# Where the split weights lie in their buffers: rows of 136 floats against rows of 128 with a start that steps

## The chip, the cores and the metric

The program runs on one core of one Trainium2 chip. The metric is the device time of one execution in microseconds; the kernel before took 2110.36 us (median of three runs, 2109.91 to 2113.37).

Names of the engines: PE is TensorE (matmuls), PEld the weight loads that it runs beside them, DVE is VectorE, ACT ScalarE, POOL GpSimd, SP SyncE, which issues the DMAs of the weights.

## What is computed

A two-layer encoder trunk on 256 tokens of width 2048, in float32. Each layer is a norm, an attention mixer with its projections, and a squared-ReLU MLP:

```python
for i in range(DEPTH):
    h = rms_norm(x, attn_norm[i])
    if i % 2 == 0:
        x = x + even_mixer(h, even_w_in[j], even_rpb[j], even_w_out[j])
    else:
        x = x + odd_mixer(h, odd_w_qkv[j], odd_sink[j], odd_w_out[j])
    x = x + sq_relu_mlp(rms_norm(x, mlp_norm[i]), w_mlp_in[i], w_mlp_out[i])
return rms_norm(x, final_norm)
```

Nearly all the work is the product of 256 tokens with weight matrices, 382 MB of which come in from HBM once.

## The kernel before

**Units.** Weights come as units of 128 output columns by 2048 inputs, in two halves of eight 128x128 blocks each. `take_half` issues the DMA of a half unit into a buffer `r` (six of them), and `split` makes two parts of it: `h`, the value rounded to float32r, by ACT (line 82), and `l = r - h`, by DVE (line 83). Each part has a pool of five buffers (`whi`, `wlo`).

**Pairs.** The activations (`u`, `hid` or `o`) are split the same way and lie as [128, k, 2, 256]: for each k the high part and behind it the low part, 2048 bytes together. `k_range` runs, for each k, one pair of matmuls into the same PSUM tile `acc`: block `h[k]` as the weights with 512 moving columns (line 150), and block `l[k]` with the 256 columns of the high part (line 152). Each matmul loads its own weights, and the load of the next runs beside the matmul before it. Pairs follow each other without a break, 16 to a unit: the projections, the MLP's two products (`hid` has 32 k for a unit of its second one), and the output projections.

**Value passes.** In `value_pair` the roles are turned: blocks of `u` are the weights, and 256 columns of `h` or `l` move (line 272), 96 matmuls to a pass and ten passes. The buffers of these half units are filled without gaps (`flat=True`).

**Rows.** All other half units are written into rows of `ROW = P + 8` = 136 floats, 544 bytes, of which 512 are used. Twelve units have the last two blocks of their second half in small tiles of their own, `hh` and `hl`, where rows of 128 floats follow each other without gaps; they belong to the two or three units that a projection begins with (`some_units`), whose last two pairs run at the end, one unit's after another's.

**Addresses.** In the built program, within a partition, `u` begins at byte 32896, `hid` and `o` at 160768, the five `h` buffers at 99744 and then every 4352 bytes, the five `l` buffers at 121504 and then every 4352, and all `hh` and `hl` tiles lie at 160 past a multiple of 256. What matters below is the place modulo 256: 128 for `u`, 0 for `hid` and `o`, 160 for every `h` and `l` buffer (4352 is 17 times 256), and the 2048-byte rows of the activations do not change it. Row k of a weight buffer begins 544k bytes in, so its place moves on by 32 with each k, and `h[k]` and `l[k]` have the same place. The **distance** of a block is its place less that of the moving operand, modulo 256: with `u` it runs 32, 64, 96 … 224, 0 over the eight k of a half unit, with `hid` and `o` it runs 160, 192, 224, 0 … 128; `hh` and `hl` stand at 32 with `u` and at 160 with `o` for both of their rows.

What sets the order: SP, ACT, DVE and PE each run their instructions as written, with `AHEAD = 2` half units loaded ahead of the one in use; attention steps are put between units by a list of tasks counted in ticks of four k.

Of the kernel before, what the change touches and what calls it, by code (L numbers as in the profile page):

```python
# [8 lines left out]
F32R = mybir.dt.float32r  # L9
# [5 lines left out]
P = 128  # L15
T = 256
# [8 lines left out]
SCALE = 128.0 ** -0.5  # L25
TW = 384
HALF = KT // 2
ROW = P + 8
RAW_BUFS = 6
PART_BUFS = 5  # L30

# [10 lines left out]
def encoder(ctx: ExitStack, tc: tile.TileContext, a: dict, outT: bass.AP):  # L42
# [4 lines left out]
    whi = ctx.enter_context(tc.tile_pool(name="whi", bufs=PART_BUFS))  # L47
    wlo = ctx.enter_context(tc.tile_pool(name="wlo", bufs=PART_BUFS))
# [32 lines left out]
    def split(hi, lo, src):  # L81
        nc.scalar.activation(hi, src, AF.Copy)  # L82
        nc.vector.tensor_sub(lo, src, hi.bitcast(F32))  # L83
# [3 lines left out]
    pending = []  # L87
    loaded = []

    def need(units, held=0, flat=False):  # L90

        for i, src in enumerate(units):
            pending.extend([(src[:, :HALF, :], HALF, flat),
                            (src[:, HALF:, :], HALF - 2 if i < held else HALF, flat)])

    def take_half():
        while pending and len(loaded) <= AHEAD:
            src, n, flat = pending.pop(0)
            r = raw.tile([P, HALF, P], F32, name="r")
            nc.sync.dma_start(r, src)  # L100
            h = whi.tile([P, HALF, ROW], F32R, name="h")
            l = wlo.tile([P, HALF, ROW], F32R, name="l")
            if flat:
                h, l = (w.rearrange("p k c -> p (k c)")[:, :HALF * P] for w in (h, l))
                split(h, l, r.rearrange("p k c -> p (k c)"))
                loaded.append((h, l, None))
                continue
            h, l = h[:, :, :P], l[:, :, :P]
            split(h[:, :n, :], l[:, :n, :], r[:, :n, :])
            tiles = [(h[:, k, :], l[:, k, :]) for k in range(n)]  # L110
            if n < HALF:
                h, l = (held_w.tile([P, 2, P], F32R, name=name) for name in ("hh", "hl"))
                split(h, l, r[:, n:, :])
                tiles += [(h[:, k, :], l[:, k, :]) for k in range(2)]
            loaded.append((h, l, tiles))
        return loaded.pop(0)

    def take_unit():
        return take_half()[2] + take_half()[2]
# [13 lines left out]
    def tick():  # L133
        now[0] += 1
        run_due()
# [49 lines left out]
    def gained(k, which):  # L185
        x, gk = xs[:, k, :], g[:, which, k:k + 1]
        if which == 4:
            nc.scalar.activation(x, x, AF.Copy, scale=gk)
        else:
            nc.scalar.activation(u[:, k, 0, :], x, AF.Copy, scale=gk)  # L190
            nc.vector.scalar_tensor_tensor(u[:, k, 1, :], x, gk, u[:, k, 0, :].bitcast(F32),
                                           op0=ALU.mult, op1=ALU.subtract)
# [68 lines left out]
    def value_pair(pool, keep):  # L261

        ps = acc_ps.tile([P, 2, T], F32, name="acc")
        for half in range(2):
            parts = [take_half()[:2] for _ in range(2)]
            for kk in range(HALF):
                k = half * HALF + kk
                h, l = (w[:, (kk % 4) * T:(kk % 4 + 1) * T] for w in parts[kk // 4])
                for j in range(2):
                    js = slice(j * P, (j + 1) * P)  # L270
                    for n, (x, y) in enumerate(((0, h), (0, l), (1, h))):
                        nc.tensor.matmul(ps[:, j, :], u[:, k, x, js], y,  # L272
                                         start=k == 0 and j == 0 and n == 0,
                                         stop=k == KT - 1 and n == 2, skip_group_check=True)
                if kk % 2 == 1:
                    tick()
        assert norm["ready"]
        w = pool.tile([P, 2, 2, T], F32R, name="v", bufs=1)
        for j in range(2):
            nc.scalar.activation(w[:, 0, j, :], ps[:, j, :], AF.Copy, scale=rcol[:, j:j + 1])  # L280
            nc.vector.scalar_tensor_tensor(w[:, 1, j, :], ps[:, j, :], rcol[:, j:j + 1],
                                           w[:, 0, j, :].bitcast(F32), op0=ALU.mult, op1=ALU.subtract)
        keep.append(w)
# [131 lines left out]
    for p in range(8):  # L415
        base = 2 * p if p < 4 else 24 + 2 * (p - 4)
        for i in range(2):
            need([w0[base + i], w0[base + 8 + i]])
        need([a["even_w_v"][p, i] for i in range(2)], flat=True)
    need([a["even_w_out"][c] for c in range(KT)], 3)  # L420

    def mlp_units(layer):
# [5 lines left out]
    mlp_units(0)  # L428
    for p in range(2):
        need([w1[NH + 2 * p + i] for i in range(2)], 2 if p == 0 else 0)  # L430
        need([a["odd_w_v"][p, i] for i in range(2)], flat=True)
        need([w1[8 * p + i] for i in range(8)])
    need([a["odd_w_out"][c] for c in range(KT)], 3)
    mlp_units(1)
# [7 lines left out]
    STARTERS = 3  # L442
# [14 lines left out]
    hl = [None] * STARTERS  # L457
    for k0, k1 in GROUPS:
        ks = slice(k0 % HALF, (k1 - 1) % HALF + 1)
        if k0 % HALF == 0:  # L460
            hl = [(whi.tile([P, HALF, ROW], F32R, name="h")[:, :, :P], wlo.tile([P, HALF, ROW], F32R, name="l")[:, :, :P])
                  for _ in range(STARTERS)]
        for i in range(STARTERS):
            split(hl[i][0][:, ks, :], hl[i][1][:, ks, :], rs[k0 // HALF][i][:, ks, :])
            if i == 0:
                for k in range(k0, k1):
                    gained(k, 0)
        for i in range(STARTERS):
            h, l = hl[i]
            for k in range(k0, k1):  # L470
                nc.tensor.matmul(sps[i], h[:, k % HALF, :], u[:, k].rearrange("p a t -> p (a t)"),
                                 start=k == 0, stop=False)
                nc.tensor.matmul(sps[i][:, :T], l[:, k % HALF, :], u[:, k, 0, :], start=False, stop=k == KT - 1)
# [12 lines left out]
    with tc.tile_pool(name="attn0", bufs=1) as pool:  # L486
# [24 lines left out]
        for p in range(8):  # L511
            q, k, v = [[], []], [[], []], []
            for i in range(2):
                for j, (dst, name, sc) in enumerate(((q, "q", SCALE), (k, "k", 1.0))):
                    done = head_parts(pool, name, 2, sc, dst[i])
                    if p == 0 and 2 * i + j < STARTERS:
                        done(sps[2 * i + j])
                    else:
                        unit(done, u)
                h = 2 * p + i  # L520
                attend(pool, o, h, q[i], k[i], v, i,
                       grid_bias(h) if h < 8 else toeplitz(pool, sl[h - 8], 1), LAGS_0)
            if p < 3:
                for h in range(2 * p + 2, 2 * p + 4):
                    make_grid_bias(h)
            value_pair(pool, v)
# [5 lines left out]
    with tc.tile_pool(name="attn1", bufs=1) as pool:  # L532
        o = pool.tile([P, NH, 2, T], F32R, name="o")
        sl = slopes(16)
        for p in range(2):
            k, v = [[], []], []
            done = [head_parts(pool, "k", 2, 1.0, k[i]) for i in range(2)]
            if p == 0:
                some_units(done, u)
                later(2, norm_for_heads)  # L540
            else:
                for i in range(2):
                    unit(done[i], u)
            value_pair(pool, v)
            for i in range(8):
                h = 8 * p + i
                q = []
                unit(head_parts(pool, "q", 2, SCALE, q), u)
                attend(pool, o, h, q, k[i // 4], v, i // 4, toeplitz(pool, sl[h], 2),
                       LAGS_1 if h < NH - 3 else LAGS_END, True)  # L550
        project_out(o, 3)
        finish_tasks()
# [87 lines left out]
```

## Time and profile before

| | us |
|---|---|
| median of 3 runs | 2110.36 |
| the profiled execution | 2113.29 |
| its span, first to last instruction | 2111.4 |
| PE busy | 2088.1 |
| DVE busy | 1339.8 |
| ACT busy | 1036.6 |

A line of the page's groups reads: source line, engine, operation, tile written <- tiles read, sizes, count, then busy time and mean duration of one. A matmul's duration runs to its modelled end and so overlaps the next one's; how fast PE goes is read from the starts. A row of the timeline begins with start and duration in us.

### The profile page before, as it was taken

The page shows a single profiled execution, that of the slowest core. Times are in us where ns is not written, and L with a number is a line of the kernel's source. Part 1 is how long each engine was busy: PE and PEld are TensorE (multiplying, and loading weights), DVE is VectorE, ACT ScalarE, POOL GpSimd, SP SyncE. Part 2 cuts the span into 40 slices and gives each one's busy share as a digit, 9 for nine tenths or more (in the row PEclk, how much of TensorE's full clock was granted, in tenths as well). Part 3 has the DMA queues.
Part 4 walks back from the last instruction along what each step waited for, and adds up shares of the span by engine and source line. Part 5 has one row for each costly group of instructions (what it writes and reads, how often), then busy time and mean ns, then how long its engine had stood idle before and what let it go on. Part 6 is the DMA issues. An engine that isn't in the chain of part 4 may idle for free.

```text
span 2111.4 us, 31825 instructions
## 1 busy us (share of the span) xinstructions
PE 2088.1 (99%) x12438; PEld 1846.7 (87%) x12438; DVE 1339.8 (63%) x2088; ACT 1036.6 (49%) x1602; POOL 23.0 (1%) x33
## 2 busy tenths in 40 slices
PE   8999999999999999999999999999999999999997
PEld 6999998888888888888889998888888888888887
DVE  6766676666655556666656877766665556665554
ACT  6555555544444444444445656554444434444442
POOL 2100000000000000000000000000000000000000
PEclk9999999999999999999999999999999999999999
DMA  9755555555555555555555454555555555555552
GB/s 260 176 174 167 168 174 174 191 185 189 189 188 189 189 189 189 190 189 190 189 189 185 149 163 144 190 185 188 189 189 189 189 189 189 189 189 190 189 189 91
DMA packets 108294, 386.06 MB, mean 183 GB/s; under 512 B 12352, under 2 KB 13392, under 8 KB 108144
## 3 DMA queue, kind: packets, MB, share of 16 engines
q1 hardware_dynamic: 106992, 381.73, 55.1%
q0 software_dynamic: 1008, 2.27, 1.5%
q8 instruction: 97, 1.59, 0.3%
q14 instruction: 53, 0.43, 0.1%
q10 hardware_dynamic: 144, 0.04, 0.0%
HBM read 381.89 MB, written 2.10 MB: 182 GB/s over the span
## 4 chain that ended last, share of the span: by engine, by line
PE 96%; DMA 2%; DVE 1%; ACT 0%; SPq 0%; issue 0%; DVEq 0%; ACTq 0%
PE acc L150 58%; PE acc L152 30%; PE acc L272 5%; PE s_ps L296 1%; PE m_ps L340 1%; DMA r<-in_even_w_in 1%; PE p_ps L321 1%; DMA r<-in_even_w_v 1%; DMA xs<-in_xT 0%; ACT h L82 0%; DVE l L83 0%; DVE xs L570 0%; PE acc L147 0%; PE acc L148 0%; PE m_ps L225 0%
## 5 line engine op out<-in xcount | busy, mean ns | idle before, releaser
L83 DVE TENSOR_TENSOR l<-r,h 128x1024 fp32r<-128x1024 f32 (+3 forms) x729 | 880.6, 1208 | 701.9 <-ACT h L82 699.3
L82 ACT ACTIVATE h<-r 128x1024 fp32r<-128x1024 f32 (+3 forms) x729 | 762.8, 1047 | 966.0 <-PE acc L150 635.9
L150 PE MATMUL acc<-u,h 128*128 128x512 f32 x2820 | 988.4, 394 | 0.0
L152 PE MATMUL acc<-u,l 128*128 128x256 f32 x2820 | 788.6, 280 | 0.0
L150 PE MATMUL acc<-hid,h 128*128 128x512 f32 x2016 | 702.4, 393 | 0.0
L150 PEld LDWEIGHTS acc<-u,h 128*128 128x128 f32 x2820 | 529.9, 188 | 119.2
L152 PE MATMUL acc<-hid,l 128*128 128x256 f32 x2048 | 572.3, 279 | 0.0
L152 PEld LDWEIGHTS acc<-u,l 128*128 128x128 f32 x2820 | 529.1, 188 | 0.2
L150 PEld LDWEIGHTS acc<-hid,h 128*128 128x128 f32 x2016 | 378.7, 188 | 87.3
L152 PEld LDWEIGHTS acc<-hid,l 128*128 128x128 f32 x2048 | 384.1, 188 | 0.0
L150 PE MATMUL acc<-o,h 128*128 128x512 f32 x500 | 175.2, 394 | 1.1 <-DVE z L181 1.1
L152 PE MATMUL acc<-o,l 128*128 128x256 f32 x500 | 139.8, 280 | 0.0
L272 PE MATMUL acc<-h,u 128*128 128x256 f32 x640 | 119.9, 283 | 0.0
L181 DVE TENSOR_TENSOR z<-acc,t 128x256 f32<-128x256 f32 x275 | 114.4, 418 | 2.2 <-ACT t L179 2.1
L150 PEld LDWEIGHTS acc<-o,h 128*128 128x128 f32 x500 | 93.9, 188 | 22.8 <-DVE z L181 1.7
L179 ACT ACTIVATE t<-acc 128x256 f32<-128x256 f32 x275 | 100.8, 367 | 5.5 <-PE acc L152 2.7
L272 PEld LDWEIGHTS acc<-h,u 128*128 128x128 f32 x640 | 101.1, 190 | 0.5
L152 PEld LDWEIGHTS acc<-o,l 128*128 128x128 f32 x500 | 93.8, 188 | 0.0
L272 PE MATMUL acc<-l,u 128*128 128x256 f32 x320 | 90.1, 281 | 0.0
L272 PEld LDWEIGHTS acc<-l,u 128*128 128x128 f32 x320 | 60.9, 190 | 0.1
L382 DVE SCALAR_TENSOR_TENSOR z<-z 128x256 f32<-128x256 f32 x128 | 54.2, 425 | 4.2
L83 DVE TENSOR_TENSOR hid<-z,hid 128x256 fp32r<-128x256 f32 x128 | 53.5, 419 | 1.3 <-ACT hid L82 1.2
(94 smaller groups left out, 857.6 us busy)
## 6 DMA issues: line engine op xcount, KB each, us to landing
r<-in_w_mlp_in SPq DMA_DIRECT2D x256, 512.0 KB, 4.5
r<-in_w_mlp_out SPq DMA_DIRECT2D x256, 512.0 KB, 4.5
r<-in_even_w_in SPq DMA_DIRECT2D x58, 512.0 KB, 4.2
r<-in_odd_w_qkv SPq DMA_DIRECT2D x40, 512.0 KB, 4.0
r<-in_even_w_v SPq DMA_DIRECT2D x32, 512.0 KB, 3.8
r<-in_even_w_out SPq DMA_DIRECT2D x32, 512.0 KB, 4.2
r<-in_odd_w_out SPq DMA_DIRECT2D x32, 512.0 KB, 3.8
r<-in_odd_w_v SPq DMA_DIRECT2D x8, 512.0 KB, 4.1
```

The costliest lines, as they stand in the source:

```text
L82: nc.scalar.activation(hi, src, AF.Copy)
L83: nc.vector.tensor_sub(lo, src, hi.bitcast(F32))
L150: nc.tensor.matmul(ps, h, act[:, k].rearrange("p a t -> p (a t)"), start=start, stop=False)
L152: nc.tensor.matmul(ps[:, :T], l, act[:, k, 0, :], start=False, stop=stop)
L179: nc.scalar.activation(t, ps[:, T:], AF.Copy)
L181: nc.vector.tensor_add(z, ps[:, :T], t)
L272: nc.tensor.matmul(ps[:, j, :], u[:, k, x, js], y, start=k == 0 and j == 0 and n == 0, stop=k == KT - 1 and n == 2, skip_group_check=True)
L296: nc.tensor.matmul(s_ps[:, i, :], qh[:, x, qs], kh[:, y, :], start=n == 0, stop=n == 2)
L321: nc.tensor.transpose(p_ps[:, j, i * P:(i + 1) * P], s[:, i, j * P:(j + 1) * P], ident)
L340: nc.tensor.matmul(o_ps[:, :T], vv[:, x, j, side * P:(side + 1) * P], pt[:, y, j, :], start=n == 0, stop=n == 5)
L382: nc.vector.scalar_tensor_tensor(z, z, 0.0, z, op0=ALU.max, op1=ALU.mult)
```

## The change

Rows lose the padding: a half unit is 1024 contiguous floats. The buffer keeps its size (1024 + 64 floats, 4352 bytes), and a half unit begins at 0, 32, 64 … or 224 bytes in it. A counter runs over all half units: `h` takes step n mod 8 and `l` step (n // 8) mod 8, so `h` moves on with every half unit, `l` with every eighth, and all 64 pairs of steps come by in turn. All eight blocks of one half unit then have one and the same distance, and `h` and `l` have two different ones, save in 8 of the 64 cases. The half units of the value passes go the same way; there the parts are the moving operand. `hh` and `hl` stay as they are.

```diff
-ROW = P + 8
+SHIFT = 8
...
+    def parts():
+
+        n = begun[0]
+        begun[0] += 1
+        out = []
+        for pool, name, at in ((whi, "h", n % 8), (wlo, "l", n // 8 % 8)):
+            w = pool.tile([P, HALF * P + 8 * SHIFT], F32R, name=name)
+            out.append(w[:, at * SHIFT:at * SHIFT + HALF * P].rearrange("p (k c) -> p k c", c=P))
+        return out
...
-            h = whi.tile([P, HALF, ROW], F32R, name="h")
-            l = wlo.tile([P, HALF, ROW], F32R, name="l")
-            if flat:
-                h, l = (w.rearrange("p k c -> p (k c)")[:, :HALF * P] for w in (h, l))
-                split(h, l, r.rearrange("p k c -> p (k c)"))
-                loaded.append((h, l, None))
-                continue
-            h, l = h[:, :, :P], l[:, :, :P]
+            h, l = parts()
             split(h[:, :n, :], l[:, :n, :], r[:, :n, :])
...
-                h, l = (w[:, (kk % 4) * T:(kk % 4 + 1) * T] for w in parts[kk // 4])
+                h, l = (w.rearrange("p k c -> p (k c)")[:, (kk % 4) * T:(kk % 4 + 1) * T] for w in parts[kk // 4])
...
-            hl = [(whi.tile([P, HALF, ROW], F32R, name="h")[:, :, :P], wlo.tile([P, HALF, ROW], F32R, name="l")[:, :, :P])
-                  for _ in range(STARTERS)]
+            hl = [parts() for _ in range(STARTERS)]
```

No engine gets an instruction more or less, and none changes its place; the buffers begin at the same bytes. What differs in the built program is the shape that the splits write, and the addresses. On ACT, in the first MLP, stood before:

```order
L82 ACTIVATE h<-r 128x8x128
L82 ACTIVATE hid<-z 128x256
L82 ACTIVATE h<-r 128x8x128
L179 ACTIVATE t<-acc 128x256
L82 ACTIVATE h<-r 128x8x128
```

and stands now:

```order
L82 ACTIVATE h<-r 128x1024
L82 ACTIVATE hid<-z 128x256
L82 ACTIVATE h<-r 128x1024
L183 ACTIVATE t<-acc 128x256
L82 ACTIVATE h<-r 128x1024
```

The same rows in the same order; a split now writes one run of 1024 floats in place of eight runs of 128.

More of the change, by code (lines that the diff above doesn't have):

```diff
@@ L88, in encoder, with need @@
     loaded = []
-    def need(units, held=0, flat=False):
+    begun = [0]
+    def parts():
[6 more added lines that the diff above has]
+        return out
+    def need(units, held=0):
         for i, src in enumerate(units):
-            pending.extend([(src[:, :HALF, :], HALF, flat),
-                            (src[:, HALF:, :], HALF - 2 if i < held else HALF, flat)])
+            pending.extend([(src[:, :HALF, :], HALF), (src[:, HALF:, :], HALF - 2 if i < held else HALF)])
     def take_half():
         while pending and len(loaded) <= AHEAD:
-            src, n, flat = pending.pop(0)
+            src, n = pending.pop(0)
             r = raw.tile([P, HALF, P], F32, name="r")
             nc.sync.dma_start(r, src)
-            h = whi.tile([P, HALF, ROW], F32R, name="h")
-            l = wlo.tile([P, HALF, ROW], F32R, name="l")
-            if flat:
-                h, l = (w.rearrange("p k c -> p (k c)")[:, :HALF * P] for w in (h, l))
-                split(h, l, r.rearrange("p k c -> p (k c)"))
-                loaded.append((h, l, None))
-                continue
-            h, l = h[:, :, :P], l[:, :, :P]
+            h, l = parts()
             split(h[:, :n, :], l[:, :n, :], r[:, :n, :])
@@ L418, in encoder @@
             need([w0[base + i], w0[base + 8 + i]])
-        need([a["even_w_v"][p, i] for i in range(2)], flat=True)
+        need([a["even_w_v"][p, i] for i in range(2)])
     need([a["even_w_out"][c] for c in range(KT)], 3)
@@ L430, in encoder @@
         need([w1[NH + 2 * p + i] for i in range(2)], 2 if p == 0 else 0)
-        need([a["odd_w_v"][p, i] for i in range(2)], flat=True)
+        need([a["odd_w_v"][p, i] for i in range(2)])
         need([w1[8 * p + i] for i in range(8)])
```

## The prediction, made before the changed kernel ran

> **What bounds the kernel now.** First the page: the busy table, the chain that ended last, and the costliest groups of PE.
>
> ```profile
> span 2111.4 us, 31825 instructions
> PE 2088.1 (99%) x12438; PEld 1846.7 (87%) x12438; DVE 1339.8 (63%) x2088; ACT 1036.6 (49%) x1602; POOL 23.0 (1%) x33
> PEclk9999999999999999999999999999999999999999
> PE acc L150 58%; PE acc L152 30%; PE acc L272 5%; PE s_ps L296 1%; PE m_ps L340 1%; DMA r<-in_even_w_in 1%; PE p_ps L321 1%; DMA r<-in_even_w_v 1%; DMA xs<-in_xT 0%; ACT h L82 0%; DVE l L83 0%; DVE xs L570 0%; PE acc L147 0%; PE acc L148 0%; PE m_ps L225 0%
> L150 PE MATMUL acc<-u,h 128*128 128x512 f32 x2820 | 988.4, 394 | 0.0
> L150 PE MATMUL acc<-hid,h 128*128 128x512 f32 x2016 | 702.4, 393 | 0.0
> L150 PE MATMUL acc<-o,h 128*128 128x512 f32 x500 | 175.2, 394 | 1.1 <-DVE z L181 1.1
> ```
>
> PE never pauses (no idle time before the pairs) at full clock, and 88% of the chain is the pairs of lines 150 and 152. With the 24 pairs on `hh` there are 2820 + 2016 + 500 + 24 = 5360 pairs. Nothing but the time of a pair, and of the 960 matmuls of line 272, can move the end by much. So the second view is the count of matmuls in a long stretch of the MLP:
>
> ```profile
> 600.00:770.00 170.00, 170.00 (x978) 148.86 (x977) 92.59 (x107) 68.83 (x76) 0.00 (x0) 1.00 0.58 189
> ```
>
> Of 978 matmuls in 170 us two only reach in from the edge; 488 pairs give **0.3484 us a pair**, and 5360 of them 1867 us. One nanosecond on a pair is 5.36 us on the kernel.
>
> Third, the timeline of PE over one half unit on `u`, k = 0 to 7, whose weights stand at distances 32, 64, 96, 128, 160, 192, 224 and 0:
>
> ```profile
> 877.08 0.39 PE L150 MATMUL acc<-u,h 128*128 128x512 f32 x1
> ...
> 877.76 0.40 PE L150 MATMUL acc<-u,h 128*128 128x512 f32 x1
> ...
> 878.47 0.39 PE L150 MATMUL acc<-u,h 128*128 128x512 f32 x1
> ...
> 879.17 0.39 PE L150 MATMUL acc<-u,h 128*128 128x512 f32 x1
> ...
> 879.87 0.39 PE L150 MATMUL acc<-u,h 128*128 128x512 f32 x1
> ```
>
> Two pairs by two, the starts lie 0.68, 0.71, 0.70 and 0.70 us apart: the work is the same in each, the time is not. The slow two are k = 2 and 3, distances 96 and 128. On `hid`, which begins 128 bytes elsewhere modulo 256, the same distances fall to k = 6 and 7; there the rows for k = 4, 6 and the next half unit's 0 read
>
> ```profile
> 655.50 0.39 PE L150 MATMUL acc<-hid,h 128*128 128x512 f32 x1
> ...
> 656.19 0.40 PE L150 MATMUL acc<-hid,h 128*128 128x512 f32 x1
> ...
> 656.90 0.39 PE L150 MATMUL acc<-hid,h 128*128 128x512 f32 x1
> ```
>
> 0.69 us for k = 4 and 5, and 0.71 for k = 6 and 7: the slow place has moved by four rows, as the distance says. So a pair's time hangs on the distance between the address that a weight load reads and the one that the matmul beside it reads. That is what the change touches, and PE has nothing to hide it behind.
>
> A rule of the Trainium skill speaks against this. SBUF — State Buffer, "Who interferes with whom", gives PE two independent read ports, one for the moving operand and one for the weights, and has it wait for nobody; by it addresses would cost nothing and the sum below would be zero. The trace does not agree with the plain form of it, since equal pairs take 0.68 to 0.71 us by twos; that the mean over distances stays can still be so, and is the first rival.
>
> **The change part by part.**
>
> The splits. They write one run where they wrote eight. Both forms are in the trace: the first row of each engine here is a half unit of a value pass, contiguous already, the second one in padded rows.
>
> ```profile
> 83.09 1.04 ACT L82 ACTIVATE h<-r 128x1024 fp32r<-128x1024 f32 x1
> 85.05 1.06 ACT L82 ACTIVATE h<-r 128x1024 fp32r<-128x1024 f32 x1 [0.92 <-ACT h L82]
> 84.16 1.23 DVE L83 TENSOR_TENSOR l<-r,h 128x1024 fp32r<-128x1024 f32 x1
> 89.47 1.23 DVE L83 TENSOR_TENSOR l<-r,h 128x1024 fp32r<-128x1024 f32 x1 [0.84 <-ACT h L82]
> ```
>
> 1.04 against 1.06 and 1.23 against 1.23 us: nothing gained. PE's work hides them in any case: ACT is busy 49% and DVE 63% of the span, and the time between two half units is 2.79 us (877.08 to 879.87). A cover that went would cost at most the 1.06 and 1.23 us of one half unit, once, at the start. No start that steps by 32 bytes is in the trace for the splits; bounded by the same rows, 0. DMAs and their queue on SP are untouched. I take 0.
>
> The pairs. Before, every half unit runs through all eight distances, `h` and `l` together. After, each block keeps its distance for eight k, and over 64 half units `h` and `l` each stand an equal time at every distance. If the cost of a matmul hung only on the distance of the weight load beside it, each distance would weigh one eighth before and after, and the sum would be **zero** exactly. It differs only if the order of distances matters: whether 32 more each time is better or worse for PE than staying.
>
> The nearest row for staying is the `hh` tiles, contiguous and at one distance, in the shape of the pairs:
>
> ```profile
> 1307.84 0.39 PE L150 MATMUL acc<-o,hh 128*128 128x512 f32 x1
> ...
> 1309.59 0.39 PE L150 MATMUL acc<-o,hh 128*128 128x512 f32 x1
> ...
> 1137.70 0.40 PE L150 MATMUL acc<-u,hh 128*128 128x512 f32 x1
> ...
> 1138.39 0.40 PE L150 MATMUL acc<-u,hh 128*128 128x512 f32 x1
> ...
> 1138.75 0.39 PE L150 MATMUL acc<-u,hh 128*128 128x512 f32 x1
> ```
>
> Five pairs on `o` (distance 160) in 1.75 us and three on `u` (distance 32) in 1.05: 0.350 us both times, **1.6 ns over the mean** of the padded rows, although in padded rows distance 32 is one of the fast two (0.68 for k = 0 and 1). The rows are good to 0.01 us, so to 2 ns on five pairs and 3 on three; the sign is likely, not certain. It is also a small sample, and the time does not settle: on `u` the first two take 0.69 together and the third alone 0.36. Only two of 64 combinations are seen, both with `h` and `l` at the same distance.
>
> Bounds: if staying cost all that these rows can hold, twice 1.6, the sum is 3.2 x 5.36 = +17.2 us. The other way I mirror half of it, −1.6 x 5.36 = −8.6 us, as no row shows staying to be cheaper for pairs but a mean cannot exclude it. The further ends, every pair as the slowest two (0.355, +35 us) or the fastest two (0.340, −45 us), are out, since all distances come by equally. Between 0 and 1.6 I take **+1.0 ns**, nearer to the rows that show staying than to the argument that it is indifferent: +5.4 us.
>
> The value passes. Their distance was one for all, 224 (weights `u` at 128, moving parts at 160); now it takes eight values in turn. The chain gives runs of line 272, and of the score matmuls, which have the same 256 moving columns at distance 0:
>
> ```profile
> 86.93 5.61 PE acc L272 x48
> 93.25 4.20 PE acc L272 x36
> 117.50 0.72 PE s_ps L296 x6
> ```
>
> 5.61 / 48 = 117 ns, 4.20 / 36 = 117 ns, against 0.72 / 6 = 120. So the place that the value passes leave was no bad one: 960 matmuls by 0 to +3 ns are 0 to +2.9 us. I take a third of the step, +1.0 us.
>
> Sum: 0 + 5.4 + 1.0 = **+6.4 us**. On the profiled execution's own 2113.29 us (span 2111.4 and 1.9 around it) that is 2119.7. That execution lies just under the slowest of the three runs shown, 2.9 over their median, and the runs are what the change is judged by, so I put the sum on the median: 2110.36 + 6.4 = 2116.8, **2117**.
>
> **Rivals.**
>
> The mean stays (no change). What costs is the distance and not its order; averaged over 64 combinations both layouts meet all distances alike, and what the `hh` rows show is their small sample. For it: the argument of equal weights, and that 0.350 lies within the reading error of 0.3484. Against it: two runs at different distances with the same excess. Pairs −0.6 to +0.6 ns: 2107 to 2114, most likely 2111. The page's rule of independent ports comes out at the same place.
>
> Staying is cheaper (faster). A stream that keeps its distance can settle into a rhythm in which the weight load and the moving operand keep out of each other's way, where one that moves on is thrown out with every block. For it: the value passes, one distance throughout, run at 117 ns where the score matmuls at another distance take 120. Against it: the `hh` rows do not settle low. It decides from −0.8 ns a pair on (−0.8 x 5.36 = −4.3 us); its price at −1.6 ns is −8.6, with +1 for the value passes 2103.
>
> That the change does not do what it says, because the pools place the buffers elsewhere, is out: buffer size and first bytes are the same in both programs.
>
> **How the numbers follow.** A measurement of this kernel tells about 0.2%, 4.2 us, from no change. Forecast, slower by 4 to 18 us: 0.50. The mean stays, within 4.2: 0.33. Faster by more: 0.17. The range leaves out a tenth at each end: down to 2104 (three quarters of the price of staying cheaper, −6.4 on 2110.4) and up to 2129 (17.2 us for the pairs and 1 for the value passes, on 2110.4). The forecast's own range is 2114.5 to 2129.
>
> **What would show it.** In the stretch from 600 to 770 us the matmuls would be 3 fewer than 978 (170 / 0.3494 is 486.5 pairs); 978 or more speaks for the rivals. Within a half unit the starts should no longer repeat the four values of the table above; half units should differ as wholes, by their pair of steps, each between 2.72 and 2.84 us (four times the fastest and the slowest two). Runs of line 272 should lie between 117 and 120 ns and differ from pass to pass. The splits should stay at 1.06 and 1.23 us, and PE's idle time before the pairs at 0. The prediction is wrong if splits grow or the order of distances turns out to help.

## The result, and the profile after

| | before | after |
|---|---|---|
| median, us | 2111.84 (4 runs, 2109.91 to 2113.37) | 2120.74 (4 runs, 2119.07 to 2122.67) |
| ratio | | 1.0043, 95% interval 1.0026 to 1.0060 |
| span of the profiled execution | 2111.4 | 2118.5 |

Slower by 0.43%, about 9 us (5.5 to 12.7 by the interval). The page of the changed kernel, in the lines that answer to those shown of before (busy table, clock, chain, groups; all source lines behind the new function have moved by three or four, so that 150 is now 154, 152 is 156 and 272 is 276):

```profile
span 2118.5 us, 31825 instructions
PE 2093.6 (99%) x12438; PEld 1851.0 (87%) x12438; DVE 1340.9 (63%) x2088; ACT 1037.3 (49%) x1602; POOL 23.3 (1%) x33
PEclk9999999999999999999999999999999999999999
PE acc L154 58%; PE acc L156 30%; PE acc L276 5%; PE s_ps L300 1%; PE m_ps L344 1%; DMA xs<-in_xT 1%; PE p_ps L325 1%; DMA r<-in_even_w_in 0%; DVE l L83 0%; DVE xs L573 0%; PE acc L474 0%; ACT h L82 0%; PE acc L152 0%; PE acc L151 0%; PE m_ps L229 0%
L83 DVE TENSOR_TENSOR l<-r,h 128x1024 fp32r<-128x1024 f32 (+3 forms) x729 | 882.3, 1211 | 703.9 <-ACT h L82 701.3
L82 ACT ACTIVATE h<-r 128x1024 fp32r<-128x1024 f32 (+3 forms) x729 | 763.0, 1047 | 967.6 <-PE acc L154 644.4
L154 PE MATMUL acc<-u,h 128*128 128x512 f32 x2820 | 991.8, 395 | 0.0
L154 PE MATMUL acc<-hid,h 128*128 128x512 f32 x2016 | 705.3, 394 | 0.0
L154 PE MATMUL acc<-o,h 128*128 128x512 f32 x500 | 175.9, 395 | 1.1 <-DVE z L185 1.1
```

Still no idle time before the pairs on `u` and `hid`, still the full clock, and ACT and DVE as busy as before. What changed is the rate. Busy times in a stretch of the MLP, where the first bracket of a row counts PE's matmuls; this is the stretch for which the prediction wanted 975 in place of 978:

```profile
600.00:770.00 170.00, 170.00 (x974) 148.83 (x973) 92.19 (x107) 68.84 (x76) 0.00 (x0) 1.00 0.58 188
```

974 matmuls are, without the two at the edges, 486 pairs: 0.3498 us a pair against 0.3484. Over all undisturbed half units (no other matmul between their eight pairs, 589 in each trace) the means are 349.88 and 348.51 ns; 1.37 ns by 5360 pairs is 7.3 us.

The second term, the value passes, stands in the chain of waits as runs of line 276 (start, length, what):

```profile
86.90 5.65 PE acc L276 x48
93.27 4.22 PE acc L276 x36
...
237.01 5.71 PE acc L276 x48
243.43 4.25 PE acc L276 x36
```

In seven passes of the first layer such 84 matmuls took 9.81 or 9.86 us before (5.61 or 5.66, and 4.20), and now 9.87 to 9.98. Over all passes the mean from start to start went from 117.1 to 118.1 ns: 960 by 1.0, 1.0 us.

And the trace holds what nobody had asked for. Two half units with the same pair of distances, `h` at 192 and `l` at 0, the first on `u`, the second on `hid`, by PE's timeline (for `u` the first pair and the last, for `hid` the first and the first of the next half unit):

```profile
214.03 0.39 PE L154 MATMUL acc<-u,h 128*128 128x512 f32 x1
...
216.41 0.39 PE L154 MATMUL acc<-u,h 128*128 128x512 f32 x1
...
664.70 0.40 PE L154 MATMUL acc<-hid,h 128*128 128x512 f32 x1
...
667.50 0.39 PE L154 MATMUL acc<-hid,h 128*128 128x512 f32 x1
```

Seven pairs in 2.38 us, 340 ns each, and eight in 2.80, 350 each, both as steady as a clock; 348.4 is the mean of the padded rows. A half unit that keeps its distances falls into a **rhythm**, and the same distances have more than one. This carries both a question (was the prediction's reason right?) and an offer (what if all pairs ran at 340?).

### The profile page after: what moved, and what is told of

Read it like the earlier page. It is cut to its first block, busy times and chain, and to the rows that moved or that the text cites. A ratio compares the mean times of both kernels' runs of the same rounds, so it can differ in the third digit from the quotient of the medians.

```text
span 2118.5 us, 31825 instructions
## 1 busy us (share of the span) xinstructions
PE 2093.6 (99%) x12438; PEld 1851.0 (87%) x12438; DVE 1340.9 (63%) x2088; ACT 1037.3 (49%) x1602; POOL 23.3 (1%) x33
## 4 chain that ended last, share of the span: by engine, by line
PE 97%; DMA 2%; DVE 1%; ACT 0%; issue 0%; SPq 0%; DVEq 0%; ACTq 0%
PE acc L154 58%; PE acc L156 30%; PE acc L276 5%; PE s_ps L300 1%; PE m_ps L344 1%; DMA xs<-in_xT 1%; PE p_ps L325 1%; DMA r<-in_even_w_in 0%; DVE l L83 0%; DVE xs L573 0%; PE acc L474 0%; ACT h L82 0%; PE acc L152 0%; PE acc L151 0%; PE m_ps L229 0%
```

## The experiments

The theory on record: PE's time per pair hangs on the distances; while a block's distance moves on by 32 with each k the pairs cost 348.5 ns in the mean, and where it stays they settle into rhythms that cost more on the whole. The rivals: the distance alone sets the cost, and its mean stays; or what costs is the stepping of the starts, or the separate places of `h` and `l`.

**Rows without padding, no steps.** The edit to the changed kernel:

```diff
-        for pool, name, at in ((whi, "h", n % 8), (wlo, "l", n // 8 % 8)):
+        for pool, name, at in ((whi, "h", 0), (wlo, "l", 0)):
```

> Rows without padding, and every half unit at the start of its buffer: h and l always at distance 32 on u and 160 on hid and o. If staying at one distance is what costs (the pairs' rhythm), this shows it without any stepping of the starts: half units at these two distances took 348 to 353.5 ns a pair in the changed kernel, about 351 in the mean, so 2.4 ns over the kernel before, some 13 us, 2124 (2110 to 2137). If the cost of the change comes from the steps of the starts (a new distance with every half unit), it is gone here: 2110 to 2114.

Measured: 2127.98 us (2124.94 to 2131.06), ratio 1.0077 (1.0062 to 1.0092). The rows of a stretch on `u` and of one on `hid`:

```profile
450.00:570.00 120.00, 120.00 (x681) 104.24 (x680) 75.73 (x108) 56.75 (x85) 0.00 (x0) 1.00 0.53 186
610.00:750.00 140.00, 140.00 (x802) 122.15 (x801) 75.70 (x87) 56.34 (x63) 0.00 (x0) 1.00 0.55 188
```

339.5 pairs in 120 us, 0.3535 us each at distance 32; 400 in 140, 0.3500 at distance 160. At these two places staying costs without any stepping, and more than the changed kernel does, so the stepping is not needed for the cost. Which places those are matters: in the changed kernel's trace the 64 pairs of distances have medians from 344.0 to 353.8 ns, and 32 with 32 (353.1) and 160 with 160 (350.7) are among the costly ones. The steps mix cheaper ones in. The `hh` rows of the prediction (0.350 at both distances) had the sign right, though not the size at 32.

**Padded rows, `l` 128 bytes from the place of `h`.** To the kernel before, a small tile between the pools, which moves `l` and all that lies behind it:

```diff
+    gap = ctx.enter_context(tc.tile_pool(name="gap", bufs=1))
     wlo = ctx.enter_context(tc.tile_pool(name="wlo", bufs=PART_BUFS))
...
+    gap.tile([P, 32], F32, name="gap")
```

> The kernel before with its padded rows, and the l buffers (and all that lies behind them) 128 bytes further: both parts move on by 32 bytes with each k as before, but l stands 128 from h's place. If moving on is what makes the kernel before cheap, nothing changes: 348.3 ns a pair give or take 1, 2105 to 2116. If it is that h and l have the same place, this costs what the change costs: about 349.8 ns a pair, 2117 to 2121.

Measured: 2114.03 us (2110.08 to 2115.31), ratio 1.0005 (0.9996 to 1.0015). The stretch on `hid`:

```profile
610.00:750.00 140.00, 140.00 (x806) 123.29 (x805) 76.20 (x87) 56.34 (x62) 0.00 (x0) 1.00 0.57 189
```

The same 806 matmuls as the kernel before has there (402 pairs, 0.3483). That `h` and `l` had equal places was not what made it cheap. Nor was it that padded rows meet other pairs of distances than the 64 of the change: in the changed kernel the undisturbed half units with `h` and `l` at equal places average 350.6 ns, and those with `l` 128 from `h` 349.7, where the padded rows, moving on, have 348.5 and 348.4 with the same two offsets. Moving on was.

**Only one part stays.** From the changed kernel, `h` contiguous and stepped, `l` in padded rows, value passes as before (their lines are left out here); and the mirror of it, with `if name == "l"`:

```diff
-        for pool, name, at in ((whi, "h", n % 8), (wlo, "l", n // 8 % 8)):
-            w = pool.tile([P, HALF * P + 8 * SHIFT], F32R, name=name)
-            out.append(w[:, at * SHIFT:at * SHIFT + HALF * P].rearrange("p (k c) -> p k c", c=P))
+        for pool, name in ((whi, "h"), (wlo, "l")):
+            if name == "h":
+                at = n % 8
+                w = pool.tile([P, HALF * P + 8 * SHIFT], F32R, name=name)
+                out.append(w[:, at * SHIFT:at * SHIFT + HALF * P].rearrange("p (k c) -> p k c", c=P))
+            else:
+                out.append(pool.tile([P, HALF, P + 8], F32R, name=name)[:, :, :P])
...
```

> Only h lies without padding and steps its start with each half unit; l keeps the padded rows of the kernel before, so its distance moves on with each k, and the value passes are as before. If a rhythm settles only where both parts stay, this is the kernel before: 348.3 ns a pair, 2108 to 2114. If it is the load of h (beside the short matmul on l) whose staying costs, it is slower like the change: about 349.8, 2116 to 2121.

> The mirror of it: l without padding and stepped, h in padded rows. By the first theory (both must stay) 2108 to 2114 again. If it is the load of l, beside the long matmul on h, whose staying costs, 2116 to 2121, and the other run is then at 2111.

Measured: `h` stays 2122.98 us, ratio 1.0048 (1.0033 to 1.0063); `l` stays 2121.11 us, 1.0040 (1.0027 to 1.0053). Neither theory in its plain form, and `h` alone came out above both of its ranges: each part alone costs as much as both, and the two do not add up. It is enough that one of the two loads stops moving on.

**The same 64 pairs in another order.** The two counters exchanged:

```diff
-        for pool, name, at in ((whi, "h", n % 8), (wlo, "l", n // 8 % 8)):
+        for pool, name, at in ((whi, "h", n // 8 % 8), (wlo, "l", n % 8)):
```

> The changed kernel with the two counters exchanged: l moves on with every half unit, h with every eighth. The same 64 pairs of distances come by equally often; only which pair follows which is another. If a half unit's time is set by its pair of distances, the mean stays 349.8 ns a pair and the kernel at 2120 (2117 to 2123), and every pair of distances has the time it had. If the rhythm also depends on where a half unit comes from, many pairs change their time (192 and 0 need not run at 340), and the mean may come out anywhere between 347 and 352: 2106 to 2132.

Measured: 2119.32 us (2117.18 to 2120.37), ratio 1.0030 (1.0018 to 1.0042). The mean over undisturbed half units is 349.6 ns, near the 349.9 of the change, but not by way of equal parts: of the 64 pairs of distances 25 moved their median by more than 1 ns, and 192 with 0 ran at 350 every time, never at 340. Which rhythm a half unit takes depends on what ran before it; the mean over many half units is about the same.

**One pair of distances throughout.** Steps chosen by the moving operand so that `h` always stands at 192 and `l` at 0; and the same for 96 and 32, which had half units of 344 and of 352 (the kind of moving operand is handed down with each unit, in lines left out here):

```diff
-        for pool, name, at in ((whi, "h", n % 8), (wlo, "l", n // 8 % 8)):
+        for pool, name, at in ((whi, "h", STEPS[kind][0]), (wlo, "l", STEPS[kind][1])):
...
+    STEPS = {"u": (5, 7), "hid": (1, 3)}
```

> Rows without padding, one fixed start for h and one for l, chosen by the moving operand so that h always stands at distance 192 and l at 0. In the changed kernel half units at this pair took either 340 ns a pair throughout (on u) or 350 throughout (on hid). If the rhythm that a half unit falls into is kept as long as nothing changes, the whole kernel runs in one of the two: about 340.5, 42 us less than before, 2068; or about 350, 10 us more, 2120. If a pair's time is an average over conflicts that the distance alone sets, u and hid differ again, and the kernel lies between, near 2095.

> The same with h at distance 96 and l at 32, for which the changed kernel shows half units of 343.9 and of 352 ns a pair, on u and on hid both. By a kept rhythm: 2086 (343.9 all along) or 2130 (352 all along), or a mixture by stretches. By distance alone one time for all half units, near 346: 2098.

Measured: 192 and 0 gave **2077.59 us** (2076.21 to 2081.82), ratio 0.9842 (0.9827 to 0.9856); 96 and 32 gave 2109.55 us, 0.9988 (0.9978 to 0.9997). Four stretches of the first of them, on `u`, `hid`, `u`, `hid` of the first MLP, by busy times:

```profile
450.00:570.00 120.00, 120.00 (x687) 105.09 (x686) 76.17 (x108) 57.93 (x86) 0.00 (x0) 1.00 0.54 189
610.00:750.00 140.00, 140.00 (x802) 122.68 (x801) 76.71 (x89) 56.66 (x64) 0.00 (x0) 1.00 0.56 188
800.00:930.00 130.00, 130.00 (x767) 114.94 (x766) 85.13 (x120) 64.35 (x97) 0.00 (x0) 1.00 0.58 194
960.00:1100.00 140.00, 140.00 (x826) 123.81 (x825) 88.50 (x118) 67.84 (x92) 0.00 (x0) 1.00 0.58 194
```

342.5 pairs in 120 us and 400 in 140 are 0.350 each; 382.5 in 130 and 412 in 140 are 0.340. The kernel neither ran in one rhythm, as the first expectation had it, nor at an average: it ran at 350 from 421 to 766 us, over the change from `u` to `hid`, and at 340 from there to the end of the first MLP. The kernel at 96 and 32 ran in stretches too, as its expectation allowed: at 352 from 433 to 776 us, and from there at 343.4 to the end of that MLP. Both write their splits in one run, as the change does, and are faster than the change, so the form of the splits is not what made the change slower. PE's timeline shows the place where the first fell out of 340:

```profile
420.20 0.39 PE L152 MATMUL acc<-u,h 128*128 128x512 f32 x1
...
420.54 0.39 PE L152 MATMUL acc<-u,h 128*128 128x512 f32 x1
...
420.88 0.50 PE L212 MATMUL m_ps<-ones,ssq 128*128 128x1 f32 x4
421.25 0.47 PE L152 MATMUL acc<-u,h 128*128 128x512 f32 x1
421.56 0.28 PE L154 MATMUL acc<-u,l 128*128 128x256 f32 x1
421.68 0.40 PE L152 MATMUL acc<-u,h 128*128 128x512 f32 x1
...
422.03 0.40 PE L152 MATMUL acc<-u,h 128*128 128x512 f32 x1
```

0.34 us from pair to pair ahead of the four small matmuls of the norm, 0.35 behind them, and the same distances all along. The second MLP, in the same trace, was entered at 350, and there the same four matmuls led the other way:

```profile
1381.16 0.40 PE L152 MATMUL acc<-u,h 128*128 128x512 f32 x1
...
1381.86 0.40 PE L152 MATMUL acc<-u,h 128*128 128x512 f32 x1
...
1382.21 0.50 PE L212 MATMUL m_ps<-ones,ssq 128*128 128x1 f32 x4
...
1384.03 0.39 PE L152 MATMUL acc<-u,h 128*128 128x512 f32 x1
...
1384.71 0.39 PE L152 MATMUL acc<-u,h 128*128 128x512 f32 x1
```

Two pairs took 0.70 us ahead of them, and 0.68 behind.

**`hh` and `hl` at these distances too.** They were a suspect, standing at 32 and 160 just ahead of that place:

```diff
-                h, l = (held_w.tile([P, 2, P], F32R, name=name) for name in ("hh", "hl"))
+                h, l = (held_w.tile([P, 2 * P + 8 * SHIFT], F32R, name=name)[:, at * SHIFT:at * SHIFT + 2 * P]
+                        .rearrange("p (k c) -> p k c", c=P) for name, at in zip(("hh", "hl"), STEPS[kind]))
...
-            t = pool.tile([P, TW], F32, name="toep", bufs=2)
+            t = pool.tile([P, TW], F32, name="toep", bufs=1)
```

> The kernel with h at 192 and l at 0 throughout, and now the hh and hl tiles at these distances too (they stood at 32, and at 160 on o), their room taken from a second buffer of the toeplitz table that one engine alone writes and reads. In the run before the first units after a projection's start, where hh and hl are used, fell out of the 340 ns rhythm and once stayed at 350 from 420 to 765 us. If it was hh and hl that threw them out, the 350 stretch goes: some 1000 pairs by 10 ns, 10 us less, 2066 to 2070. If it is the wait itself (PE stops there for the norm), the rhythm is drawn anew at each such stop and this lands anywhere from 2066 to 2090.

Measured: 2090.92 us (2090.28 to 2093.12), ratio 0.9898 (0.9882 to 0.9915): worse than without it. PE now fell to 350 behind the norm's matmuls in both MLPs, at 424 and at 1383 us, and stayed there to 769 and 1728. So `hh` and `hl` were not the cause; the interruption is. Nor does it look like chance: in the traces of the four kernels with 192 and 0 (the one before, this one and the two that follow) the norm's four matmuls in an MLP exchanged the rhythm all eight times, from 340 to 350 six times and from 350 to 340 twice. This kernel lost because it came to both norms at 340, the one before only to the first. It is no general rule: at 96 and 32 the same four left 344 as it was, and the norm's next interruption, at 433 us, turned it into 352.

**A nudge.** If the rhythm is a state, 16 pairs at other distances should be able to change it. In the fifth unit of each MLP the two halves get `h` at 128 and 160 with `l` at 0, the way that had led to 340 in the changed kernel; the second kernel has 64 for the first half alone:

```diff
-    STEPS = {"u": (5, 7), "hid": (1, 3)}
+    STEPS = {"u": (5, 7), "hid": (1, 3), 0: (3, 7), 1: (4, 7)}
...
+            if b == 0:
+                for half in range(2):
+                    pending[half - 56] = pending[half - 56][:2] + (half,)
```

> The kernel with h at 192 and l at 0 throughout (hh and hl left at their old places), but the two halves of the fifth unit of each MLP have h at 128 and then at 160, l at 0: the distances that stood ahead of 192 and 0 where the changed kernel ran at 340 on u. In the run without it PE fell into 350 ns a pair at the stop before that unit (at 420 us) and stayed so to 765. If a rhythm is a state that only a changed distance or a stop can alter, these 16 pairs of 5360 draw it anew: either 340 from there on in the first MLP, 10 us less, 2066 to 2069; or 350 again, 2077 (or, if the second MLP, which ran at 340, is thrown out of it, 2087). If what held the 350 stretch was something of that stretch itself (its data, its DMAs), nothing changes: 2077.

> The same with another disturbance: the first half of that unit has h at distance 64, l at 0, the second none. At the step from hid to u one load of h stands at distance 64 and the rhythm came out at 340, from 350 and from 340 alike. If that is what does it: 2066 to 2069. If the rhythm is drawn without regard to it: 2077 or 2087.

Measured: the first one **2071.95 us** (2069.67 to 2075.55), ratio 0.9808 (0.9788 to 0.9827), the best of all; the second one 2078.88 us, 0.9854 (0.9807 to 0.9902). The first one's stretches on `u` and `hid`:

```profile
450.00:570.00 120.00, 120.00 (x708) 106.17 (x707) 78.35 (x111) 59.41 (x89) 0.00 (x0) 1.00 0.56 194
610.00:750.00 140.00, 140.00 (x825) 123.90 (x825) 78.91 (x91) 58.01 (x65) 0.00 (x0) 1.00 0.57 194
```

353 pairs in 120 us and 411.5 in 140: 0.340. In this run PE fell to 350 at the norm in both MLPs (at 420 and 1370 us), and both times ran at 340 from the nudge on, at 435 and 1384, to the end of the MLP. The second nudge did not do it: in the first MLP PE was at 340 ahead of it (it had come to the norm at 350) and stayed there, in the second it was at 350 and stayed at 350 to 1717. For the first nudge the expected 2066 to 2069 was somewhat low; why is not shown. Only one execution of each kernel has a trace, and the rhythms of the others are not known: the four times with the second nudge run from 2076.02 to 2094.07 us.

## Why the prediction was right

The sum was +6.4 us on 2110.36, 2117, with slower as the likeliest outcome (0.50). Measured were 2120.74 us and a difference of 5.5 to 12.7 by the interval; the fourth run of the kernel before moved its own median by 1.5 us.

- **Pairs, +1.0 ns, +5.4 us.** Measured 1.4 ns and 7.3 us, the larger part of the difference. The reason given, that staying at a distance costs more than moving on, held in the mean over the 64 pairs of distances: 349.9 against 348.5 ns. It does not hold at every place, as 192 with 0 shows. The size lay between 0 and 1.6 as taken, nearer to the `hh` rows than the prediction put it. Here was luck: those rows stood at two places that are both costly to stay at, and a row at 224 with 224 (median 347.1 in the changed kernel) would have given the other sign.
- **Value passes, +1.0 us.** Measured 1.0 ns on 960 matmuls. The three kernels that left them at distance 224 (no steps, and only one part staying) kept 117 ns.
- **Splits, 0.** On whole half units (702 each) 1228 against 1226 ns on DVE, and 1061 against 1061 on ACT.
- **That the distance sets a pair's time** the trace of the kernel before shows more sharply row by row than two by two: over k = 0 to 7 the pairs on `u` take 344, 343, 354, 355, 345, 353, 347 and 348 ns in the mean, and those on `hid` the same series four rows later, within 1 ns. The slow places are 96 and 128, as the prediction read, and also 192 (k = 5), which its sums of two hid.
- **The rival that the mean stays** fell for this change, though it is right for padded rows: there the two places of `l` give 348.5 and 348.4 ns over all undisturbed half units. The Trainium skill (SBUF — State Buffer, "Who interferes with whom") gives PE two independent read ports and has it wait for nobody. The conclusion that the prediction drew from this, that addresses cost nothing, does not hold here: the kernel with the first nudge differs from the kernel before in where its weights lie and in the form of the splits, which cost the same, and is 1.9% faster. Whether it is at the ports that the time goes, no run shows.
- **The rival that staying is cheaper** fell as a forecast of this change, but not as a mechanism: the quiet rhythm it spoke of exists, 340 ns, and the change visited it only in 5 of some 620 half units.
- **What was wrong though the time was right:** "half units should differ as wholes, by their pair of steps". They differ by pair of steps and by what ran before them; all but five of the 589 lie within the 2.72 to 2.84 us that it gave. And the `hh` rows at distance 32 read 0.350, where staying there for long costs 0.3535.

The spans differ by 7.1 us and the two terms give 8.3. Of the −1.2 between them, 0.7 is made up behind the last pair, which begins 7.8 us later than before (2086.2 and 2094.0 us); the rest was not split.

Not settled: why PE has such rhythms. That a load of weights and the moving operand beside it get in each other's way at certain distances fits all runs, but no run shows where in the memory or in PE the time goes; that stepping through the places averages 349.6 to 350.3 ns, above the 348.5 of moving on, is a measured mean and not derived; and what decides which rhythm follows an interruption is open.

## What to carry to other kernels

Where PE is never idle and equal matmuls still follow each other at unequal times, look at their starts one by one: a period in them that follows a buffer's rows points at the addresses, and a layout is worth a survey, since one kernel that steps through all places shows in one trace which may be cheap. Judge a place in a kernel that holds it throughout, and look behind each interruption, as a rhythm outlives the cause that set it and two copies of one loop can run 3% apart. In these runs padding that makes the distance move on gave a steady mean, 348.4 to 348.5 ns with either place of `l`; a fixed distance gave anything from 1.6% less time (192 and 0, without a nudge) to 0.8% more (no steps).

## What the runs showed of the hardware

- The time of a 512-column and a 256-column float32r matmul, each with its own weight load, ran from 340 ns (192 and 0) to 357 (only `l` staying) in the mean of a half unit, a few beside interruptions left out, at one and the same granted clock (1.00 in the stretches shown). It follows the distance modulo 256 between the addresses that the load and the matmul read, and what ran before.
- At one pair of distances (192 and 0) there are two steady rhythms, 340 and 350 ns; each was kept for hundreds of microseconds, 350 from 421 to 766, across a change of the moving operand. Four matmuls of one column exchanged them eight times of eight; 16 pairs at other distances turned 350 into 340 both times, and 8 pairs at another did not.
- It takes only one of the two loads to stay at its distance: 1.0048 for `h` alone, 1.0040 for `l` alone, 1.0043 for both.
